# A decoder block's first stage in four groups of 256 tokens instead of two of 512, with plain fp32 projections

## The chip, the cores and the metric

The kernel runs on one core of one Trainium2 chip. The metric is device time in microseconds (us), the median of several timed runs. Beside them one execution was recorded by the hardware profiler; all rows below come from that one.

## What is computed

For 1024 tokens of 1024 features, in fp32 (the weights are drawn at random; shapes matter here, not values):

```
h    = modulate(rms_norm(x), shift1, scale1)      # shift, scale, gate: six rows made from c @ w_ada
q_g,k_g,v_g,a,r_g,q_s,k_s,v_s = split(h @ w_in)   # 1024 -> 2320 columns
o_gla = gated linear attention(q_g,k_g,v_g,a), normed, * silu(r_g)
o_swa = sliding-window attention(q_s,k_s,v_s), 8 heads, window 128, normed
x    = x + gate1 * (concat(o_gla,o_swa) @ w_out)
h2   = modulate(rms_norm(x), shift2, scale2)
for each of 8 heads of q = h2 @ w_q:               # 1024 -> 2048 columns
    16 best of 128 keys in each half, 16 best of their sums -> 16 experts e, gates g = softmax
a    = gelu(h2 . u_tab[e]);  out = sum_e g * a * v_tab[e]      # 128 experts of 16384 per token
x    = x + gate2 * out;  result = rms_norm(x) * final_g
```

## The kernel before

Tokens are held in 8 blocks of 128. The work has two stages.

**First stage** (`prelude(g)`, a generator with two `yield`s, so in three parts). It is run for two groups of 512 tokens (`GT`, `GB = 4` blocks). Part 1 normalises x, transposes it to `hT` and projects it. Part 2 is both attentions (`level`, `swa`), the v and r projections, the out-projection (`w_out`) and h2 with its transpose `h2T`. Part 3 multiplies by `w_q` and picks the 16 best experts of each head (`sel_head`, VectorE instructions L536 to L540, sums on GpSimd L552), then decodes them to expert numbers (`sel_decode4`).

Weights arrive in chunks of 256 columns, four tiles of 256 KB each (`load_chunk`). Two forms of product are in use. In group 0, and for `w_q` in both groups, the weights and `hT` are split into two fp32r parts (tile `whl`, made by ScalarE, VectorE and GpSimd at L165 and L166) and each product is three matmuls (`mm3`, L174 to L176). The other products of group 1 are one plain fp32 matmul on the tile as loaded (`wful`, L184 and L195). `proj_T` keeps the weights stationary and streams all tokens of the group (512 columns), `proj_tok` keeps 128 tokens stationary and streams 256 weight columns.

**Second stage** (the experts). Blocks 0 to 3 are *gathered*: for each of 128 slots, GpSimd gathers one row of `u` per token (512 KB, L631), VectorE takes the dot product with the token's row `h2s` (L632, tile `acts`); then one row of `v` per slot, which is either added up on VectorE (`gather_v`, L645 and L647) or contracted on TensorE (`gather_vt`, L699 and L674, tile `py`). The token rows come from DRAM: h2 is spilled to `h2d`, read back, transposed to `h2r`, and read from there. All gathered rows share the pool `gp` of seven 4 KB buffers. Blocks 4 to 7 are *dense*: all 16384 experts are computed for their 512 tokens in 128 tiles (`dense_u`: tiles `ur`, `uh`, matmuls `da`; `dense_w`, `dense_v`: tiles `wl`, `vl`, matmuls `dv` and `keep`) with a gate matrix that `build_gates` makes first (tile `st`, matmuls `gt`). 31 of the 128 `da` tiles are made ahead, some before and some during `build_gates`, and kept in DRAM (`gad`).

**What sets the order.** The program is written as one sequence: group 0; part 1 and 2 of group 1; u of block 0; v of block 0 with u of block 1; part 3 of group 1; `da` tiles; gates; v of 1 with u of 2; v of 2 with u of 3; v of 3; finish; dense loop. A scheduler then places the instructions of all engines by priority, so later work moves up beside earlier work; on each engine the order is fixed when the program is built.

Of the kernel before, what the change touches and what calls it, by code (L numbers as in the profile page):

```python
# [34 lines left out]
GBUF = 7  # L35
# [7 lines left out]
def hymba_peer_kernel(ctx, tc, x, c, w_adaT, b_adaT, g1T, g2T, w_in, w_alpha, b_alphaT,  # L43
# [56 lines left out]
    def row_of(dst, part):  # L100
        rep = wt("rep", [128, 8, 128], "e", 2)
# [12 lines left out]
    def late_consts():  # L114
# [8 lines left out]
        t = wt("lvlf", [128, NL, 128], "e", 2)  # L123
# [29 lines left out]
    def load_chunk(src, ci):  # L153
        res = []
        if busy[0] and src is not w_q:
            for kq in range(4):
                raw = wp.tile([128, 2, 256], F, name="wful", tag="whl", bufs=5)
                last_load[0] = SP.dma_start(raw, src[ci, kq // 2][:, kq % 2 * 2:kq % 2 * 2 + 2])
                res.append(raw)
            return res  # L160
        for kq in range(4):
            raw = wp.tile([128, 2, 256], F, name="wraw", tag="wraw", bufs=3)
            last_load[0] = SP.dma_start(raw, src[ci, kq // 2][:, kq % 2 * 2:kq % 2 * 2 + 2])
# [6 lines left out]
    busy = [False]  # L170
# [18 lines left out]
    def proj_tok(ch, hT, b, evac):
        p = pst("pK", "pj")  # L190
        for k in range(8):
            wk = ch[k // 2]
            ts = slice(b * 128, b * 128 + 128)
            if wk.dtype == F:
                PE.matmul(p[:, :256], lhsT=hT[:, k, ts], rhs=wk[:, k % 2], start=k == 0, stop=k == 7)  # L195
                continue
            mm3(p[:, :256], (hT[:, 0, k, ts], hT[:, 1, k, ts]), (wk[:, 0, k % 2], wk[:, 1, k % 2]), k == 0, k == 7)
        evac(p[:, :256])

    def transpose_split(blocks, hT, k, mul, add=None, spill=None, kind="ps", full=False):  # L200

        p = pst("tr", kind)
        for i, a in enumerate(blocks):
            PE.transpose(p[:, i * 128:(i + 1) * 128], a, ident)
        if full:
            if add is None:
                A.activation(hT[:, k], p, AF.Copy, scale=mul)
            else:
                A.activation(hT[:, k], p, AF.Identity, scale=mul, bias=add)
            return  # L210
        t = w2.tile([128, GT], F, name="trt", tag="w2")
# [624 lines left out]
    with ExitStack() as pre:  # L836
# [8 lines left out]
        for _ in prelude(0):  # L845
            pass
# [118 lines left out]
```

## Time and profile before

| | us |
|---|---|
| timed runs, median (lowest to highest of 3) | 2974.2 (2973.9 to 2984.5) |
| profiled execution, its own time | 2984.96 |
| span of its instructions | 2983.2 |
| TensorE (PE) busy / VectorE (DVE) busy | 2550.9 / 2342.1 |
| GpSimd (POOL) / ScalarE (ACT) busy | 1645.1 / 968.3 |
| granted TensorE clock, mean share | 0.917 |

Two kinds of view matter below. A table of stretches gives for each stretch of time the busy time of every engine: the stretch less PE's busy time is PE's idle time. A table of groups gives the price of one kind of instruction. The stretches were cut where the stages change: group 0's attention and out-projection end at about 335 us, its expert choice at 500; group 1's attention ends at about 860 and its choice at 1110; the gates are built from 1190 to 1494; the dense loop runs from 1560 to 2825.

### The profile page before, as it was taken

What the parts mean: (1) busy time and instruction counts of PE and PEld (TensorE: products, weight loads), DVE (VectorE), ACT (ScalarE), POOL (GpSimd) and SP (SyncE); (2) the same over time, 40 slices, a digit from 0 to 9 for tenths busy, and PEclk for the clock granted to TensorE, in tenths of its full rate; (3) what the DMA queues carried; (4) which work ended last, traced back from release to release, by engine and by line L of the source; (5) the groups of instructions that cost most, each with busy time, mean ns of one, the idle gap of its engine ahead of it and who ended that gap; (6) DMA issues with size and microseconds to landing.
All of it is one profiled execution on the core that took longest, in us unless ns stands there. A gap on an engine that the chain in (4) does not pass through costs nothing. (4 is left out here: it accounts for less than half of the span.)

```text
span 2983.2 us, 37273 instructions
## 1 busy us (share of the span) xinstructions
PE 2550.9 (86%) x12528; PEld 1960.1 (66%) x12528; DVE 2342.1 (79%) x5034; ACT 968.3 (32%) x1837; POOL 1645.1 (55%) x1551
## 2 busy tenths in 40 slices
PE   5799898898789873899769999999999999999800
PEld 4588775576566551688647777777888788877600
DVE  7754499899769999788846665666888888898987
ACT  4444533223132121577822222222222222222101
POOL 2321363678778888543244545454555555555675
PEclk9899999996889885999979999999999999999955
DMA  9502422689998787988798989998999999999897
GB/s 329 174 30 75 158 73 71 207 295 321 339 371 283 264 310 240 363 307 334 311 369 328 349 328 326 362 332 312 376 340 339 345 344 342 337 341 336 297 357 289
DMA packets 280657, 865.21 MB, mean 290 GB/s; under 512 B 28544, under 2 KB 69776, under 8 KB 278416
## 3 DMA queue, kind: packets, MB, share of 16 engines
q0 software_dynamic: 150192, 546.90, 50.6%
q1 hardware_dynamic: 122288, 271.10, 25.5%
q10 hardware_dynamic: 7984, 44.83, 3.8%
q8 instruction: 98, 1.61, 0.2%
q14 instruction: 95, 0.78, 0.1%
HBM read 806.36 MB, written 56.89 MB: 289 GB/s over the span
## 5 line engine op out<-in xcount | busy, mean ns | idle before, releaser
L631 POOL DMA_INDIRECT u<-in_peer_u_dram,exi x512 | 640.5, 1251 | 419.9 <-DVE acts L632 112.9
L632 DVE CUSTOM_DVE_ANT_0 u<-u,h2s 128x1024 f32<-128x1024 f32 x512 | 636.0, 1251 | 105.3 <-DMA u<-in_peer_u_dram,exi 64.7
L699 POOL DMA_INDIRECT v<-in_peer_v_dram,exs x256 | 300.7, 1175 | 278.0 <-DVE acts L632 137.2
L645 POOL DMA_INDIRECT v<-in_peer_v_dram,exi x256 | 332.0, 1297 | 219.8 <-DVE acts L632 124.1
L174 PE MATMUL da<-h2T,uh 128*128 128x512 f32 x1024 | 407.2, 398 | 6.3 <-ACT ga L781 6.0
L176 PE MATMUL da<-h2T,uh 128*128 128x512 f32 x1024 | 407.6, 398 | 4.6 <-DVE uh L775 4.4
L175 PE MATMUL da<-h2T,uh 128*128 128x512 f32 x1024 | 405.9, 396 | 0.0
L647 DVE SCALAR_TENSOR_TENSOR yacc<-v,gates,yacc 128x1024 f32<-128x1024 f32 x254 | 325.9, 1283 | 14.1 <-DMA v<-in_peer_v_dram,exi 10.8
L174 PE MATMUL dv<-vl,wl 128*128 128x512 f32 x640 | 251.4, 394 | 9.7 <-ACT vl L803 9.2
L176 PE MATMUL dv<-vl,wl 128*128 128x512 f32 x640 | 250.8, 392 | 0.0
L175 PE MATMUL dv<-vl,wl 128*128 128x512 f32 x640 | 249.6, 392 | 0.3 <-DVE vl L804 0.3
L822 DVE TENSOR_TENSOR acc<-dv,acc 128x512 f32<-128x512 f32 x155 | 105.1, 687 | 170.9 <-PE dv L176 153.3
L176 PEld LDWEIGHTS da<-h2T,uh 128*128 128x128 f32 x1024 | 194.4, 190 | 62.8 <-issue 12.6
L174 PEld LDWEIGHTS da<-h2T,uh 128*128 128x128 f32 x1024 | 194.7, 190 | 59.0 <-ACT ga L781 10.7
L175 PEld LDWEIGHTS da<-h2T,uh 128*128 128x128 f32 x1024 | 194.3, 190 | 51.4 <-issue 10.9
L674 PE MATMUL py<-v,wz 128*32 128x512 f32 x1024 | 152.0, 668 | 81.4 <-DMA v<-in_peer_v_dram,exs 81.3
L803 ACT ACTIVATE vl<-vr 128x1024 fp32r<-128x1024 f32 x128 | 132.8, 1051 | 251.9 <-PE dv L176 228.4
L774 ACT ACTIVATE uh<-ur 128x1024 fp32r<-128x1024 f32 x128 | 135.0, 1055 | 217.2 <-PE da L176 164.6
L781 ACT ACTIVATE ga<-da 128x512 f32<-128x512 f32 x128 | 76.0, 594 | 387.4 <-PE da L176 339.0
L166 POOL TENSOR_TENSOR whl<-wraw,whl 128x512 fp32r<-128x512 f32 x76 | 105.1, 1389 | 147.5 <-ACT whl L165 143.9
L775 DVE TENSOR_TENSOR uh<-ur,uh 128x1024 fp32r<-128x1024 f32 x128 | 162.1, 1267 | 26.9 <-ACT uh L774 22.8
L804 DVE TENSOR_TENSOR vl<-vr,vl 128x1024 fp32r<-128x1024 f32 x128 | 155.6, 1219 | 27.9 <-ACT vl L803 26.6
(278 smaller groups left out, 5435.9 us busy)
## 6 DMA issues: line engine op xcount, KB each, us to landing
ur<-in_peer_uT_dram SPq DMA_DIRECT2D x128, 512.0 KB
vr<-in_peer_v_dram SPq DMA_DIRECT2D x128, 512.0 KB
gd<-st ACTq DMA_DIRECT2D x16, 2048.0 KB
gl<-gd SPq DMA_DIRECT2D x32, 1024.0 KB
wada<-in_w_adaT_dram SPq DMA_DIRECT2D x48, 512.0 KB
wraw<-in_w_q_dram SPq DMA_DIRECT2D x64, 256.0 KB
wraw<-in_w_in_dram SPq DMA_DIRECT2D x40, 256.0 KB
wful<-in_w_in_dram SPq DMA_DIRECT2D x40, 256.0 KB
```

The costliest lines, as they stand in the source:

```text
L174: PE.matmul(p, lhsT=lh[0], rhs=rh[0], start=first, stop=False)
L175: PE.matmul(p, lhsT=lh[0], rhs=rh[1], start=False, stop=False)
L176: PE.matmul(p, lhsT=lh[1], rhs=rh[0], start=False, stop=last)
L631: GP.indirect_dma_start(out=u, out_offset=None, in_=peer_u, in_offset=bass.IndirectOffsetOnAxis(ap=exi[:, j:j + 1], axis=0))
L632: V.tensor_tensor_reduce(out=u, in0=u, in1=h2s, scale=1.0, scalar=0.0, op0=AL.mult, op1=AL.add, accum_out=a[:, j:j + 1])
L645: GP.indirect_dma_start(out=v, out_offset=None, in_=peer_v, in_offset=bass.IndirectOffsetOnAxis(ap=exi[:, j:j + 1], axis=0))
L647: V.scalar_tensor_tensor(out=y, in0=v, scalar=wg[:, j:j + 1], in1=y, op0=AL.mult, op1=AL.add)
L674: m = PE.matmul(py[q:q + 32, :], lhsT=wz[:, j, i % 8 * 32:i % 8 * 32 + 32], rhs=vs[j][:, hf * 512:hf * 512 + 512], start=i == 0, stop=i == 31)
L699: gi = GP.indirect_dma_start(out=v, out_offset=None, in_=peer_v, in_offset=bass.IndirectOffsetOnAxis(ap=exs[:, t:t + 1], axis=0))
L774: A.activation(hl[:, 0], u, AF.Copy)
L775: V.tensor_tensor(hl[:, 1], u, hl[:, 0], AL.subtract)
L804: V.tensor_tensor(vl[:, 1], v, vl[:, 0], AL.subtract)
```

## The change

Groups are now of 256 tokens (`GB = 2`), so the first stage runs four times (p0 to p3), each with all weights loaded again. All its products are plain fp32: `load_chunk` keeps the loaded tile (six buffers), the split and its three-matmul form remain only in the dense stage. The gathered blocks are 0, 1 (from p0) and 6, 7 (from p3), the dense ones 2 to 5 (p1 and p2), whose split `h2D` is written as soon as h2 is there. The token rows of gathered blocks stay in SBUF (`h2rows`, two buffers); `h2d` and `h2r` are gone. `gp` has six buffers. The order is a list: `PLAN` (p is the next part of a group, d decodes, u gathers u, w is `gather_vt`, a6 six `da` tiles), and after the gates `POST` (x is `gather_v`). `finish` is as before, for blocks 0, 1, 6, 7.

```diff
-GT = 512
-GB = GT // 128
-NG = S // GT
-
-D0 = 4
+
+GB = 2
+GT = GB * 128
+
+D0 = 2
 ND = 4
...
-GBUF = 7
+GBUF = 6
...
     def load_chunk(src, ci):
...
         for kq in range(4):
-            raw = wp.tile([128, 2, 256], F, name="wraw", tag="wraw", bufs=3)
-            last_load[0] = SP.dma_start(raw, src[ci, kq // 2][:, kq % 2 * 2:kq % 2 * 2 + 2])
-            hl = wp.tile([128, 2, 2, 256], R, name="whl", tag="whl", bufs=5)
-            A.activation(hl[:, 0], raw, AF.Copy)
-            (GP if kq % 2 or (not busy[0] and src is w_q) else V).tensor_tensor(hl[:, 1], raw, hl[:, 0], AL.subtract)
-            res.append(hl)
+            w = wp.tile([128, 2, 256], F, name="wful", tag="w", bufs=6)
+            last_load[0] = SP.dma_start(w, src[ci, kq // 2][:, kq % 2 * 2:kq % 2 * 2 + 2])
+            res.append(w)
...
     def proj_T(ch, hT, mt, evac):
-        p = pst("pT", "pj")
+        p = pst("pT", "pj")[:, :GT]
         for k in range(8):
...
-            mm3(p, (wk[:, 0, k % 2, cs], wk[:, 1, k % 2, cs]), (hT[:, 0, k], hT[:, 1, k]), k == 0, k == 7)
+            PE.matmul(p, lhsT=ch[k // 2][:, k % 2, mt * 128:mt * 128 + 128], rhs=hT[:, k], start=k == 0, stop=k == 7)
...
-        for blk in range(D0):
-            h2 = gp.tile([128, 8, 128], F, name="h2l", tag="g")
-            SP.dma_start(h2, h2d[:, :, blk * 128:blk * 128 + 128].rearrange("k p t -> p k t"))
-            h2s = gp.tile([128, D], F, name="h2t", tag="g")
+    def token_rows(h2T, g):
+
+        for b in range(GB):
+            h2s = h2rows[g * GB + b] = sm.tile([128, D], F, name="h2s", tag="h2s", bufs=2)
...
+    PLAN = "p0 p0 p0 p1 d0 p1 u0 w0 p1 p2 d1 p2 u1 p2 p3 d2 p3 p3 d3 a6".split()
+    POST = "w1 u6 x6+u7 x7".split()
...
-    run(gather_vt(1, sels[1]), gather_u(2, sels[2]))
-    run(gather_v(2, sels[2]), gather_u(3, sels[3]))
-    run(gather_v(3, sels[3]))
-    for b in range(D0):
+    for op in POST:
+        run(*(GATHER[o[0]](int(o[1:]), sels[int(o[1:])]) for o in op.split("+")))
+    for b in GATHERED:
         finish(None, b, GP)
```

Two places show what the scheduler made of it. The first is GpSimd where the gathers of u begin. In the rows before, `cand` is part of the expert choice, `oh` of the decoding, `e` of an attention level, `h2s` the load of the token rows.

```order
91 L552 TENSOR_TENSOR cand<-tv 128x16 x50
92 L576 TENSOR_TENSOR oh<-oh,dif 128x1024
...
96 L627 DMA h2s<-h2r 128x1024
97 L576 TENSOR_TENSOR oh<-oh,idf 128x1024
98 L576 TENSOR_TENSOR oh<-oh,dif 128x1024 x2
99 L576 TENSOR_TENSOR oh<-oh,idf 128x1024
100 L322 TENSOR_TENSOR e<-bcum 128x8x64
101 L322 TENSOR_TENSOR e<-bcum 128x16x32
102 L325 TENSOR_TENSOR e<-e,kg 128x8x64
103 L325 TENSOR_TENSOR e<-e,kg 128x16x32
104 L631 DMA u<-in_peer_u_dram,exi 128x1024 x9
```

The same place now:

```order
38 L532 TENSOR_TENSOR cand<-tv 128x16 x28
39 L556 TENSOR_TENSOR oh<-oh,dif 128x1024
40 L556 TENSOR_TENSOR oh<-oh,idf 128x1024
41 L298 TENSOR_TENSOR e<-bcum 128x4x64
42 L298 TENSOR_TENSOR e<-bcum 128x8x32
43 L556 TENSOR_TENSOR oh<-oh,dif 128x1024
44 L556 TENSOR_TENSOR oh<-oh,idf 128x1024
45 L607 DMA u<-in_peer_u_dram,exi 128x1024 x4
46 L301 TENSOR_TENSOR e<-e,kg 128x4x64
47 L607 DMA u<-in_peer_u_dram,exi 128x1024 x2
```

Before, 160 `cand` rows (the choice for 512 tokens) stand ahead of the first gather; now 80 do (256 tokens), and the gathers begin in the second group's attention as they did before, only that this group comes earlier.

The second place is VectorE at the end of the program, where `yacc` adds one gathered row of v, `acc` belongs to the dense loop and `ga`, `wl`, `vl` prepare its last tiles. Before:

```order
3613 L804 TENSOR_TENSOR vl<-vr,vl 128x1024
3614 L647 SCALAR_TENSOR_TENSOR yacc<-v,gates,yacc 128x1024
3615 L822 TENSOR_TENSOR acc<-dv,acc 128x512 x2
3616 L647 SCALAR_TENSOR_TENSOR yacc<-v,gates,yacc 128x1024 x3
3617 L822 TENSOR_TENSOR acc<-dv,acc 128x512
...
3621 L822 TENSOR_TENSOR acc<-dv,acc 128x512
3622 L647 SCALAR_TENSOR_TENSOR yacc<-v,gates,yacc 128x1024 x80
3623 L725 TENSOR_TENSOR yl<-yl,rows 128x1024
```

and now:

```order
3591 L772 TENSOR_TENSOR ga<-gl,ga 128x512
3592 L623 SCALAR_TENSOR_TENSOR yacc<-v,gates,yacc 128x1024
3593 L775 TENSOR_TENSOR wl<-ga,wl 128x512
3594 L623 SCALAR_TENSOR_TENSOR yacc<-v,gates,yacc 128x1024 x4
3595 L798 TENSOR_TENSOR acc<-dv,acc 128x512 x2
3596 L623 SCALAR_TENSOR_TENSOR yacc<-v,gates,yacc 128x1024 x4
3597 L798 TENSOR_TENSOR acc<-dv,acc 128x512
3598 L623 SCALAR_TENSOR_TENSOR yacc<-v,gates,yacc 128x1024 x2
3599 L798 TENSOR_TENSOR acc<-dv,acc 128x512
3600 L701 TENSOR_TENSOR yl<-yl,rows 128x1024
3601 L623 SCALAR_TENSOR_TENSOR yacc<-v,gates,yacc 128x1024
3602 L798 TENSOR_TENSOR acc<-dv,acc 128x512
```

Eighty gathered rows stood behind the last instruction of the dense loop; now twelve stand behind the last `ga`, among the loop's last additions.

## Rows read from the trace of the kernel before

**Rows 1.** The page: busy time; DMA share in 40 slices; bytes moved.

```profile
PE 2550.9 (86%) x12528; PEld 1960.1 (66%) x12528; DVE 2342.1 (79%) x5034; ACT 968.3 (32%) x1837; POOL 1645.1 (55%) x1551
DMA  9502422689998787988798989998999999999897
DMA packets 280657, 865.21 MB, mean 290 GB/s; under 512 B 28544, under 2 KB 69776, under 8 KB 278416
```

**Rows 2.** Stretches: start:end, length, busy time (instructions) by engine, clock, DMA.

```profile
core 0: us, PE busy (x) PEld busy (x) DVE busy (x) ACT busy (x) POOL busy (x), PEclk, DMA share, GB/s
0.00:45.00 45.00, 15.24 (x59) 12.07 (x60) 32.59 (x50) 23.67 (x36) 18.04 (x17) 1.00 0.83 303
45.00:335.00 290.00, 257.28 (x1711) 221.19 (x1710) 164.52 (x362) 129.60 (x306) 75.79 (x57) 0.92 0.39 133
335.00:500.00 165.00, 149.38 (x681) 118.94 (x682) 144.34 (x801) 64.40 (x121) 86.29 (x194) 0.93 0.25 82
500.00:566.00 66.00, 57.20 (x153) 25.97 (x151) 58.38 (x126) 20.02 (x32) 34.90 (x23) 0.95 0.42 135
566.00:860.00 294.00, 251.82 (x1237) 194.70 (x1237) 239.57 (x516) 77.43 (x217) 221.81 (x178) 0.83 0.90 321
860.00:1110.00 250.00, 219.30 (x1042) 152.21 (x1042) 231.34 (x902) 73.78 (x129) 210.30 (x278) 0.92 0.85 297
1110.00:1190.00 80.00, 29.71 (x122) 11.52 (x123) 73.78 (x174) 8.86 (x30) 66.53 (x56) 0.53 0.72 241
1190.00:1494.00 304.00, 276.54 (x1734) 221.80 (x1732) 248.83 (x679) 211.75 (x490) 117.81 (x99) 0.97 0.87 330
1494.00:1560.00 66.00, 38.28 (x167) 24.85 (x166) 32.20 (x48) 13.86 (x20) 31.80 (x27) 0.74 0.97 373
1560.00:2825.00 1265.00, 1256.13 (x5637) 976.84 (x5635) 983.64 (x1266) 335.88 (x444) 676.46 (x528) 1.00 0.92 337
2825.00:2983.00 158.00, 0.00 (x0) 0.00 (x0) 132.92 (x115) 9.06 (x16) 105.38 (x98) 0.50 0.88 322
```

**Rows 3.** Order of time on DVE: start, length, instruction; the last gathered rows.

```profile
2937.75 2.61 DVE L647 SCALAR_TENSOR_TENSOR yacc<-v,gates,yacc 128x1024 f32<-128x1024 f32 x2 [0.21 <-DMA v<-in_peer_v_dram,exi]
```

**Rows 4.** One stretch, instructions with tile whl alone: PE, PEld, DVE, ACT, POOL.

```profile
0.00:1560.00 1560.00, 378.85 (x1848) 296.44 (x1848) 33.94 (x44) 74.03 (x120) 105.08 (x76) 0.89 0.69 248
```

**Rows 5.** The same stretch, tile wful alone: PE, PEld.

```profile
0.00:1560.00 1560.00, 213.90 (x720) 138.75 (x720) 0.89 0.69 248
```

**Rows 6.** Groups: names, shapes, count | busy us, mean ns | idle before, releaser.

```profile
L195 PE MATMUL pK<-wful,hT 128*128 128x256 f32 x320 | 85.0, 412 | 1.3 <-DVE pa L265 1.3
L184 PE MATMUL pT<-hT,wful 128*128 128x512 f32 x144 | 65.6, 607 | 8.8 <-ACT qs L304 7.3 <-ACT kg L278 1.5
L195 PE MATMUL pK<-wful,cT 128*128 128x256 f32 x256 | 63.3, 401 | 8.2 <-DVE y L492 6.4 <-DMA wful<-in_w_out_dram 1.6 <-issue 0.2
L525 PE MATMUL sk<-kk,qT 128*128 128x128 f32 x256 | 42.5, 290 | 12.3 <-ACT s L527 9.9 <-ACT qT L521 2.3
L674 PE MATMUL py<-v,wz 128*32 128x512 f32 x1024 | 152.0, 668 | 81.4 <-DMA v<-in_peer_v_dram,exs 81.3
L774 ACT ACTIVATE uh<-ur 128x1024 fp32r<-128x1024 f32 x128 | 135.0, 1055 | 217.2 <-PE da L176 164.6 <-DMA ur<-in_peer_uT_dram 37.4 <-DVE acc L822 14.3
L775 DVE TENSOR_TENSOR uh<-ur,uh 128x1024 fp32r<-128x1024 f32 x128 | 162.1, 1267 | 26.9 <-ACT uh L774 22.8 <-ACT whl L165 2.9 <-issue 1.0
```

**Rows 7.** Order of time on PE: a run of 256-column fp32 matmuls.

```profile
776.91 1.89 PE L195 MATMUL pK<-wful,cT 128*128 128x256 f32 x8
```

**Rows 8.** A stretch of split 256-column matmuls, tile whl alone.

```profile
280.00:325.00 45.00, 42.66 (x363) 41.56 (x362) 4.28 (x5) 7.21 (x12) 9.84 (x7) 1.00 0.40 136
```

**Rows 9.** The choice of group 1, instructions with tile u alone: DVE, POOL.

```profile
860.00:1110.00 250.00, 69.90 (x53) 60.61 (x52) 0.92 0.85 297
```

**Rows 10.** DMA issues: a weight tile's size.

```profile
wful<-in_w_out_dram SPq DMA_DIRECT2D x16, 256.0 KB
```

More of the change, by code (lines that the diff above doesn't have):

```diff
@@ L22 @@
 NB = S // 128
-GT = 512
-GB = GT // 128
-NG = S // GT
-D0 = 4
+GB = 2
+GT = GB * 128
+D0 = 2
 ND = 4
 DT = ND * 128
+GATHERED = [b for b in range(NB) if not D0 <= b < D0 + ND]
 NGA = NB - ND
@@ L187, in proj_T @@
         evac(p)
     def proj_tok(ch, hT, b, evac):
-        p = pst("pK", "pj")
+        p = pst("pK", "pj")[:, :256]
         for k in range(8):
[L192 to L197, printed above, removed]
@@ L198, in proj_tok, with transpose_to @@
-        evac(p[:, :256])
-    def transpose_split(blocks, hT, k, mul, add=None, spill=None, kind="ps", full=False):
-        p = pst("tr", kind)
+            PE.matmul(p, lhsT=hT[:, k, b * 128:b * 128 + 128], rhs=ch[k // 2][:, k % 2], start=k == 0, stop=k == 7)
+        evac(p)
+    def transpose_to(blocks, hT, k, mul, add=None, split=None, kind="ps"):
+        p = pst("tr", kind)[:, :GT]
         for i, a in enumerate(blocks):
             PE.transpose(p[:, i * 128:(i + 1) * 128], a, ident)
[L205 to L211, printed above, removed]
@@ L212, in transpose_split @@
         if add is None:
-            A.activation(t, p, AF.Copy, scale=mul)
+            A.activation(hT[:, k], p, AF.Copy, scale=mul)
         else:
-            A.activation(t, p, AF.Identity, scale=mul, bias=add)
-        A.activation(hT[:, 0, k], t, AF.Copy)
-        V.tensor_tensor(hT[:, 1, k], t, hT[:, 0, k], AL.subtract)
-        if spill is not None:
-            SP.dma_start(spill, t)
+            A.activation(hT[:, k], p, AF.Identity, scale=mul, bias=add)
+        if split is not None:
+            A.activation(split[:, 0, k], hT[:, k], AF.Copy)
+            V.tensor_tensor(split[:, 1, k], hT[:, k], split[:, 0, k], AL.subtract)
@@ L248, in prelude @@
                     mod_in(k)
-                transpose_split([xn[b][:, k * 128:(k + 1) * 128] for b in range(GB)], hT, k, A1[:, k:k + 1], modT[:, k:k + 1], kind="lv", full=g > 0)
+                transpose_to([xn[b][:, k * 128:(k + 1) * 128] for b in range(GB)], hT, k, A1[:, k:k + 1], modT[:, k:k + 1], kind="lv")
         qg = wt("qg", [128, 2, GT])
@@ L500, in prelude @@
             A.activation(ys[b], ys[b], AF.Copy, scale=rsqrt_of(ss, D, "n2"))
-        h2T = hx.tile([128, 2, 8, GT], R, name="h2T", tag="hT")
+        h2T = Parts([wt("h2T", [128, 2, GT], tag, n) for tag, n in (("ST0", 1), ("ST1", 1), ("e", 2), ("e", 2))])
+        dense = D0 <= g * GB < D0 + ND
+        split = h2D[:, :, :, (g * GB - D0) * 128:(g * GB - D0) * 128 + GT] if dense else None
         for k in range(8):
-            transpose_split([ys[b][:, k * 128:(k + 1) * 128] for b in range(GB)], h2T, k, A2[:, k:k + 1], modT[:, 24 + k:25 + k], None if g else h2d[k])
+            transpose_to([ys[b][:, k * 128:(k + 1) * 128] for b in range(GB)], h2T, k, A2[:, k:k + 1], modT[:, 24 + k:25 + k], split)
+        if not dense:
+            token_rows(h2T, g)
         if g == 0:
-            t = wt("g2row", tag="e", bufs=2)
+            t = wt("g2row", tag="oh", bufs=2)
             row_of(t, 5)
@@ L532, in prelude @@
         res[g] = sels
-        h2Ts[g] = h2T
     def top16(s, v, i, n):
@@ L886, in hymba_peer_kernel @@
         build_gates(lists)
-        lq.close()
-        for i in tiles[N1:]:
+        for i in tiles:
             ahead(i)
+    dq.close()
+    lq.close()
+    du = ctx.enter_context(tc.tile_pool(name="du", bufs=2, side="right", reuse_waits="tile"))
     dv = ctx.enter_context(tc.tile_pool(name="dv", bufs=1, reuse_waits="tile"))
```

175 lines of the change are left out of this document (80 added, 95 removed).

## The prediction

> **What bounds the kernel now.** I read the page's totals first, then the stretches, then the prices of single instructions. TensorE is the busiest engine with 2550.9 us, VectorE follows with 2342.1, and the DMA engines are seven to nine tenths busy from the ninth of 40 slices on, after an early hole [rows 1]. No engine is full over the whole span, so the stretches decide [rows 2]. In the dense loop (1560 to 2825) PE is idle for 9 us of 1265: there PE sets the pace. Behind it lie 158 us without one matmul. Gathered rows are still being added there; the last two end at 2940.4 [rows 3], and some 43 us of finishing follow. Ahead of the loop PE is idle for 265 us, spread over all stages. So the profiled time, 2985.0, is PE's work (2551), plus its idle time before its last matmul (9 + 265 = 274), plus the tail (158), plus 2 around the span. I predict each of these. The profiled execution is 10.7 us above the median of the timed runs, 2974.2; I sum on the former and subtract 10.7.
>
> **PE's work.** In the built programs `da`, `dv`, `keep`, `gt`, `py`, transposes and attention matmuls are the same in number (3072, 1920, 1152, 512, 512 for the first five); only the projections change. Removed: 378.9 us of split matmuls [rows 4] and 213.9 us of plain ones [rows 5], 593 together. Added: 1376 plain fp32 matmuls of 256 columns. Their prices: 85.0 us for 160 of them with `hT` gives 0.531 each, 63.3 for 128 with `cT` 0.495 (each leaves two records, so x320 is 160) [rows 6]. 320 with `hT` make 170 us and 256 with `cT` 127. The other 800 are `proj_T` at 256 columns, which no row shows. Half of its 512-column price (65.6 / 72 = 0.911) is 0.456, the lower end; 0.531 is the upper end, since the columns are the same. I take 0.495, the row between: 396 us (365 to 425). Sum 693 (662 to 722), so PE's work grows by **100 us** (69 to 129).
>
> A clean run of four such matmuls takes 1.89 us, 0.47 each [rows 7]; a split one of 256 columns takes 42.66 / 363 = 0.118 per matmul, 0.353 for three [rows 8]. The Trainium skill, FP8 and Floating Point Precision, TensorE Precision Notes, says that true fp32 goes through the array in four passes; four times 0.118 is 0.47, so the trace agrees, and the rule speaks against this change. By the rule alone the 1376 would take 647 us and the work would grow by 54 instead of 100. I keep the rows, which hold the gaps of a real stage.
>
> **The tail.** VectorE's order now leaves 12 gathered additions behind the last `ga`, among the loop's last `acc`, where 80 stood behind the last `acc`. Then the same finishing follows as before, 43 us, of which the loop's last additions hide nothing. I take 45 for 158: **-113 us**. Bounds: 30, if dense finishing overlaps the gathered one, and 120, if some 50 gathers are late at (2940.4 - 2825) / 80 = 1.45 us each.
>
> **PE's idle time, stage by stage** [rows 2]. In us, before and then after:
> Start (0 to 45): 30, then 30; the same 16 tiles of `w_ada` must land.
> Group 0 (45 to 335): 33, then 17, as it is half the attention.
> Its expert choice (335 to 500): 16, then 8.
> Projections of the next group (500 to 566): 9, then 9.
> Attention beside gathers (566 to 860): 42; then the same density of gathers, for 512 tokens in p1 and p3 (72 and 81 of u in VectorE's order), 45, and p2, which has none of u, as group 0, 17: 62.
> Choice of group 1 beside gathers (860 to 1110): 31. This is now the dearest point. A choice for 512 tokens keeps VectorE busy for 144.3 us of 165 (335 to 500), so 72 for 256. One u costs it 69.90 / 53 = 1.32 us [rows 9]. The order puts 56 of u between the last out-projection and the last choice of p1, and 47 in p3: 146 and 134 us on VectorE. PE has 128 matmuls at 0.495, 32 scores at 42.5 / 128 = 0.33 [rows 6] and some transposes, 78 us. It waits for VectorE through the five buffers of the scores (tile `s`), so it can be five of the 16 score blocks ahead, 45 and 42 us; in these it makes the next projections, or `da` tiles, which stand next in its queue. Idle then 23 and 14; without any lead 68 and 56. p2 has only w0 beside it (PE 108, VectorE 72): 8. I take 57 (45 to 132).
> Decoding (1110 to 1190): 50, then 0. The lists of the dense blocks now come with d1 and d2, hidden by the attention of p2 and p3; d3 is hidden by six `da` tiles. Without that cover it is 25 for two blocks.
> Gates (1190 to 1494): 27, then 30. The 81 us for which PE waits on gathered v [rows 6] fall mostly here and in the row before last; w1 now runs alone and GpSimd is not held by u, so I take half of them, 14 of 27, away. The six `da` tiles have one buffer each, so the split of the next tile is not hidden behind the last: 6 times 1.06 + 1.27 us [rows 6] and a little, 16.
> Change of pools (1494 to 1560): 28, then 28. Dense loop: 9, then 9.
> The sums are 275 and 250: **-25 us** (-37 to +75).
>
> **Edits that I cost at nothing.** The splits (74 us ACT, 105 POOL, 34 DVE [rows 4]) go, on engines with room beside PE. 176 more weight tiles of 256 KB [rows 10] are 46 MB; at 337 GB/s 137 us of DMA, hidden in p0 and p1, where the DMA engines are 0.25 to 0.42 busy [rows 2]. The first gather comes at about 45 + 145 + 83 (start, half of two stretches) + 25 (a quarter of the fp32 growth) + 30 for decoding = 330 us. Without that cover: of 865 MB [rows 1] + 46 - 8 for the spill that is gone, about 850 come after it (48 tiles of `w_ada` and p0's weights lie ahead); at 337 GB/s they end at 2850, some 90 us before the forecast's end. Six instead of seven row buffers: GpSimd's 528 instructions in the loop, nearly all gathers, are one per 2.4 us, so six buffers leave 14 us for each row; nothing, or up to 20.
>
> **Sum.** 2985.0 + 100 - 113 - 25 = 2947, less 10.7: **2936 us**. Its own range, 2890 to 2985, holds the prices' bounds and the ordinary scatter of the idle terms.
>
> **The rivals.**
> *Starved in the choice* (slower). PE has no lead in p1 and p3, because the next instructions in its queue wait for VectorE too, and stands there for 68 + 56 + 8 = 132 instead of 57. With d3 uncovered (+25) and 0.531 for the 800 (+29) the time is 2936 + 75 + 25 + 29 = 3065; without the last two 3011. It is slower from about 2936 + 38, so once these stages leave PE idle for over 95 us. For it: in 1110 to 1190 PE was idle 50 of 80 us behind VectorE. Against it: in 860 to 1110, with 53 of u beside the choice [rows 9], PE was 88% busy [rows 2].
> *The gaps close* (faster). Waits for gathered v and decoding made 131 of the 274; if both go wholly and p1 to p3 run as tightly as group 0, idle falls to 180: 2866. For it: w0 and w1 run alone. Against it: the same u stand beside half as many columns per stage.
> *Late rows.* The dense loop ends but gathers don't: 50 left cost 75 us more than my tail, 3011. For it: VectorE's order has 500 rows in the loop, and the DMA share there was 0.92. Against it: the old loop carried 528 instructions of GpSimd with PE at 99% [rows 2].
>
> **How the numbers follow.** Forecast 0.52, starved 0.20, gaps close 0.16, late rows 0.12. A measurement can't tell less than 0.5%, 15 us, from no change. Of the forecast's 0.52 some 0.36 lie below 2959, 0.13 within 15 us of 2974, 0.03 above; so faster 0.36 + 0.16 + a little of the others' low ends, 0.54; same 0.16; slower 0.30. The range reaches into the rivals: 2862 to 3035.
>
> **What would show it.** PE busy at about 2650 and `wful` at about 693 us; the first u near 330 us; no stretch like 1110 to 1190; PE's last matmul within 50 us of the end; idle in the choices of p1 and p3 of 40 us. I am wrong if PE's work grows by over 130, if these choices leave PE idle for over 95 us, or if rows are still gathered well after the last matmul.

## The result, and the profile after

The changed kernel took 2937.35 us (median of 4 runs, 2932.59 to 2944.7), the kernel before 2974.82 in the same session: a ratio of 0.987, with an interval of 0.984 to 0.990. Forecast were 2936 us. The profiled execution took 2935.2 us with a span of 2933.4. It splits into TensorE's work 2618.0, its idle time before the last matmul 270.7, the tail 44.7 and 2 around the span. Before, these were 2551, 274, 158 and 2.

The page's totals of the kernel after, to be held against [rows 1]:

```profile
PE 2618.0 (89%) x12704; PEld 2061.1 (70%) x12704; DVE 2270.2 (77%) x5027; ACT 942.6 (32%) x1844; POOL 1567.0 (53%) x1499
...
DMA  9533689979987999778898989999999999999986
```

TensorE has 67 us more work, VectorE 72 less, and the early hole in the DMA row is shorter. The stretches of the same kernel, with the columns of [rows 2]: the start; then, for each of the four groups in turn, the stretch up to the end of its out-projection and the stretch of its choice (eight rows); gates; change of pools; dense loop; tail.

```profile
0.00:45.00 45.00, 17.57 (x50) 12.08 (x51) 26.80 (x47) 18.15 (x29) 14.31 (x13) 0.92 0.93 331
45.00:197.00 152.00, 139.19 (x721) 113.62 (x720) 83.23 (x201) 47.64 (x131) 15.87 (x19) 0.96 0.57 204
197.00:284.00 87.00, 77.19 (x403) 67.73 (x403) 52.52 (x290) 28.61 (x64) 22.59 (x62) 0.94 0.41 135
284.00:470.00 186.00, 157.79 (x747) 126.10 (x745) 155.25 (x427) 48.44 (x130) 119.80 (x118) 0.86 0.78 270
470.00:570.00 100.00, 73.75 (x357) 62.83 (x358) 88.27 (x348) 30.65 (x71) 69.42 (x92) 0.86 0.96 347
570.00:792.00 222.00, 191.39 (x1085) 126.17 (x1083) 122.79 (x380) 57.01 (x157) 147.20 (x162) 0.94 0.87 308
792.00:904.00 112.00, 101.12 (x541) 66.38 (x538) 68.89 (x374) 30.71 (x68) 68.27 (x120) 0.93 0.84 304
904.00:1084.00 180.00, 157.13 (x777) 125.47 (x776) 156.49 (x358) 49.75 (x136) 138.19 (x112) 0.88 0.87 306
1084.00:1193.00 109.00, 78.72 (x376) 66.76 (x376) 92.22 (x353) 22.18 (x52) 74.20 (x99) 0.86 0.90 322
1193.00:1627.00 434.00, 380.63 (x2257) 275.24 (x2257) 287.32 (x843) 243.60 (x537) 188.39 (x186) 0.94 0.83 304
1627.00:1670.00 43.00, 24.30 (x75) 18.08 (x76) 21.97 (x33) 8.18 (x12) 15.55 (x13) 0.70 1.01 392
1670.00:2889.00 1219.00, 1219.00 (x5327) 1000.61 (x5325) 1081.60 (x1347) 348.54 (x448) 675.10 (x487) 1.00 0.93 336
2889.00:2934.00 45.00, 0.24 (x2) 0.00 (x0) 32.82 (x36) 9.19 (x16) 18.15 (x18) 0.53 0.59 208
```

The first column less the second is TensorE's idle time of a stretch. The loop begins 110 us later than before (1670 for 1560), takes 46 less, and only 45 us follow it for 158. (Before, 59.7 us of `py` matmuls stood in the loop; now none do.) The choices of groups 1 and 3 (470 and 1084) leave TensorE idle for 26.3 and 30.3 us. Where in them, the order of time on TensorE tells, group 1 first (start, length, instruction, idle time before it and what ended it):

```profile
488.54 0.90 PE L188 MATMUL tr<-ident,y 128*128 128x128 f32 x3 [18.85 <-ACT y L477]
...
1104.24 0.90 PE L188 MATMUL tr<-ident,y 128*128 128x128 f32 x3 [20.72 <-ACT y L477]
```

Two waits make 39.6 of the 56.6 us. They stand before the choice begins: the out-projection is done and the normalised rows `y` are not there. What is late is seen on VectorE, and on SyncE's queue, both between 461 and 482:

```profile
469.38 0.43 DVE L470 TENSOR_TENSOR y<-y,xr 128x256 f32<-128x256 f32 x1 [2.17 <-DMA xr<-in_x_dram]
...
471.54 0.47 DVE L470 TENSOR_TENSOR y<-y,xr 128x256 f32<-128x256 f32 x1
...
476.51 0.08 DVE L608 DVE_READ_ACCUMULATOR2_ANT acts<- 128x1 f32 x1
481.23 0.43 DVE L470 TENSOR_TENSOR y<-y,xr 128x256 f32<-128x256 f32 x1 [4.64 <-DMA xr<-in_x_dram]
```

```profile
461.87 6.20 SPq L153 DMA_DIRECT2D wful<-in_w_q_dram  x4
469.84 0.33 SPq L468 DMA_DIRECT2D xr<-in_x_dram  x1
470.22 0.42 SPq L153 DMA_DIRECT2D wful<-in_w_q_dram  x1
472.04 0.33 SPq L468 DMA_DIRECT2D xr<-in_x_dram  x1
```

VectorE adds the slice `xr` of the residual at 481.23, after waiting for it. `xr` has two buffers, and the two last slices were asked for at 469.84 and 472.04, just when the additions of the two slices before them were done (469.81 and 472.01). Five weight tiles of 256 KB for the next projections had been asked for ahead of the first, a sixth ahead of the second. The first slice was used 11.4 us after it was asked for, the second landed after 12.3. The DMA engines are 96% busy in the stretch from 470 to 570. From the addition to the scaled `y` another 7 us pass.

The projections after, by shape (to [rows 4 to 6]; their sum over the first 1700 us is 681.4):

```profile
L175 PE MATMUL pT<-h2T,wful 128*128 128x256 f32 x1024 | 249.7, 391 | 0.1
...
L181 PE MATMUL pK<-wful,hT 128*128 128x256 f32 x640 | 164.7, 406 | 2.8 <-ACT hT L192 2.8
...
L175 PE MATMUL pT<-hT,wful 128*128 128x256 f32 x576 | 142.5, 405 | 16.5 <-ACT kg L254 7.8 <-ACT qs L280 4.1 <-DMA wful<-in_w_in_dram 2.7
...
L181 PE MATMUL pK<-wful,cT 128*128 128x256 f32 x512 | 124.6, 397 | 7.9 <-DVE y L469 6.7 <-DMA wful<-in_w_out_dram 1.0
```

Halved counts give 0.488 us (249.7 / 512), 0.515, 0.495 and 0.487 for one matmul; the forecast had 0.495 for the `pT`, 0.531 and 0.495 for the `pK`.

### The profile page after: what moved, and what is told of

It is laid out like the page before. It is cut to its first block, busy times and chain, and to the rows that moved or that the text cites. A ratio compares the mean times of both kernels' runs of the same rounds, so it can differ in the third digit from the quotient of the medians.

```text
span 2933.4 us, 37844 instructions
## 1 busy us (share of the span) xinstructions
PE 2618.0 (89%) x12704; PEld 2061.1 (70%) x12704; DVE 2270.2 (77%) x5027; ACT 942.6 (32%) x1844; POOL 1567.0 (53%) x1499
## 4 chain that ended last, share of the span: by engine, by line
PE 67%; DVE 15%; DMA 8%; issue 4%; POOL 3%; ACT 2%; SPq 0%; POOLq 0%; ACTq 0%; DVEq 0%
PE da L162 8%; PE da L160 8%; PE da L161 8%; PE dv L160 5%; PE dv L161 5%; PE dv L162 5%; PE pK L181 5%; PE pT L175 4%; DVE u L608 4%; PE gt L738 3%; PE py L650 3%; PE keep L160 3%; PE keep L161 3%; PE keep L162 3%; DMA v<-in_peer_v_dram,exs 2%
## 5 line engine op out<-in xcount | busy, mean ns | idle before, releaser
L607 POOL DMA_INDIRECT u<-in_peer_u_dram,exi x512 | 652.4, 1274 | 453.9 <-DVE acts L608 316.1
L621 POOL DMA_INDIRECT v<-in_peer_v_dram,exi x256 | 366.5, 1432 | 288.4 <-DVE yacc L623 233.9
L162 PE MATMUL da<-h2D,uh 128*128 128x512 f32 x1024 | 410.7, 401 | 28.1 <-DVE uh L751 28.1
L160 PE MATMUL da<-h2D,uh 128*128 128x512 f32 x1024 | 412.0, 402 | 9.8 <-ACT uh L750 9.8
L675 POOL DMA_INDIRECT v<-in_peer_v_dram,exs x256 | 261.5, 1022 | 295.7 <-PE py L650 236.2
L161 PE MATMUL da<-h2D,uh 128*128 128x512 f32 x1024 | 410.3, 401 | 0.0
L162 PEld LDWEIGHTS da<-h2D,uh 128*128 128x128 f32 x1024 | 196.8, 192 | 79.1 <-DVE uh L751 32.6
L175 PE MATMUL pT<-h2T,wful 128*128 128x256 f32 x1024 | 249.7, 391 | 0.1
L160 PEld LDWEIGHTS da<-h2D,uh 128*128 128x128 f32 x1024 | 197.1, 192 | 61.0 <-ACT uh L750 13.8
L161 PEld LDWEIGHTS da<-h2D,uh 128*128 128x128 f32 x1024 | 196.9, 192 | 48.4 <-issue 6.7
L175 PEld LDWEIGHTS pT<-h2T,wful 128*128 128x128 f32 x1024 | 192.8, 197 | 30.3 <-issue 7.5
L774 ACT ACTIVATE wl<-ga 128x512 fp32r<-128x512 f32 x128 | 80.0, 626 | 336.1 <-PE dv L162 249.0
L650 PE MATMUL py<-v,wz 128*32 128x512 f32 x1024 | 141.8, 624 | 29.6 <-DMA v<-in_peer_v_dram,exs 29.6
L738 PEld LDWEIGHTS gt<-o,o 128*128 128x128 f32 x1024 | 132.4, 198 | 50.1 <-issue 16.3
L181 PE MATMUL pK<-wful,hT 128*128 128x256 f32 x640 | 164.7, 406 | 2.8 <-ACT hT L192 2.8
## 6 DMA issues: line engine op xcount, KB each, us to landing
gd<-st ACTq DMA_DIRECT2D x16, 2048.0 KB, 15.5
```

The costliest lines, as they stand in the source:

```text
L160: PE.matmul(p, lhsT=lh[0], rhs=rh[0], start=first, stop=False)
L161: PE.matmul(p, lhsT=lh[0], rhs=rh[1], start=False, stop=False)
L162: PE.matmul(p, lhsT=lh[1], rhs=rh[0], start=False, stop=last)
L175: PE.matmul(p, lhsT=ch[k // 2][:, k % 2, mt * 128:mt * 128 + 128], rhs=hT[:, k], start=k == 0, stop=k == 7)
L181: PE.matmul(p, lhsT=hT[:, k, b * 128:b * 128 + 128], rhs=ch[k // 2][:, k % 2], start=k == 0, stop=k == 7)
L607: GP.indirect_dma_start(out=u, out_offset=None, in_=peer_u, in_offset=bass.IndirectOffsetOnAxis(ap=exi[:, j:j + 1], axis=0))
```

## The experiments

All times are medians. "The changed kernel" is 2937.35 us; the kernel before took 2974.82 to 2983.6 beside these runs, and each ratio is to it as run beside them. TensorE's idle time is that before its last matmul, and the tail what follows; both, and TensorE's work, are of the run's profiled execution. The kernel before took about 2975 us beside `xr4`, `xract`, `a0`, `gbuf5` and the changed kernel itself, and 2981 to 2984 beside the others, so a difference between runs of the two sets is sure to some 10 us only; the ratios show it without this shift.

**Four buffers for the slices** (`xr4`):

```diff
-                xt = wt("xr", [128, 256], "xr", 2)
+                xt = wt("xr", [128, 256], "xr", 4)
-        ex = w2.tile([128, 128], F, name="ex", tag="ex", bufs=2)
+        ex = w2.tile([128, 128], F, name="ex", tag="ex", bufs=1)
```

> The changed kernel with four buffers instead of two for the residual slices `xr` (the space comes from one buffer of the small list `ex`). Theory 1 (late slices): the 18.9 and 20.7 us for which TensorE stands before the transposes of `y` at the end of groups 1 and 3 come from slices that are asked for behind five weight tiles; with four buffers they are asked for two steps earlier, the two gaps fall to about 4 us each and TensorE's idle time from 271 to about 240. VectorE's order has 6 gathered additions behind the last `acc` where the changed kernel has none, so the tail grows from 44 to about 54: some 2915 in all. Theory 2 (VectorE): the gaps stay, since dots of `u` stand ahead of the norm in VectorE's order; idle above 260, time 2930 to 2940. Theory 3 (rows set the end): idle falls by 30 and the tail grows by as much, because the loop starts earlier with more rows left; 2930 to 2940 with another split.

Measured: 2920.1 us (0.982, 0.979 to 0.985), 17 less than the changed kernel. VectorE no longer waits for `xr` at all, but the gaps ahead of `tr` fell only to 14.2 and 10.7: another wait stood behind the first. The order of time on TensorE, and on ScalarE:

```profile
482.69 0.90 PE L188 MATMUL tr<-ident,y 128*128 128x128 f32 x3 [14.18 <-ACT y L477]
```

```profile
481.49 1.15 ACT L477 ACTIVATE y<-y,n2r 128x1024 f32<-128x1024 f32 x1 [10.43 <-DMA x1d<-y]
```

ScalarE scales `y` in place and must wait until its store to `x1d` has read it; that store was issued at 469 behind six weight tiles. Idle time fell by 7 (forecast 31), the tail grew by 11 (forecast 10). The choices of groups 1 and 3 had 24 us less idle time, but nearly as much came back at the six early `da` tiles, which waited longer for VectorE's halves:

```profile
1164.61 0.80 PE L162 MATMUL da<-h2D,uh 128*128 128x512 f32 x1 [12.32 <-DVE uh L751]
...
1203.69 0.79 PE L162 MATMUL da<-h2D,uh 128*128 128x512 f32 x1 [29.13 <-DVE uh L751]
```

What made the run faster is TensorE's work, 2596.5 for 2618.0, which no theory had; the last section says where such differences come from. So theory 1 holds for the wait for `xr` and for the tail, not for the gaps, the idle time and the source of the gain.

**The slices on another queue** (`xract`):

```diff
-                with tc.issue_after(last_load[0].ins):
-                    SP.dma_start(xt, x[...])
+                    A.dma_start(xt, x[...])
```

> The changed kernel with `xr` loaded by ScalarE's queue instead of SyncE's, two buffers as before. If standing in SyncE's queue behind the weight tiles makes the slices late, the two gaps before the transposes of `y` fall from 18.9 and 20.7 to under 10 each and the time by 15 to 25, to about 2915. If the full DMA engines (share 0.96 to 0.97 there) or the two buffers make them late, the gaps stay within 5 us and the time within 8 of 2937.

Measured: 2950.0 us (0.991, 0.988 to 0.994), 13 more than the changed kernel and outside the forecast of either case; the gaps were 18.7 and 16.6, as the second case has them. The slices of group 1 were again asked for only when the additions two steps before were done (472.27 and 473.80, after 471.85 and 473.66), so the two buffers and not the queue set when they are asked for. What they then waited for the run doesn't separate: VectorE's recorded waits for `xr` fell from 15.2 us to 0.3, but its order had more dots of `u`, waiting for rows themselves, ahead of the addition, which came at 481.09 for 481.23. The Trainium skill, DMA: Bandwidth & Descriptors, Issuing engines are not separate DMA queues, says that transfers of all issuing engines run interleaved on the same 16 DMA engines; the nearly unchanged gaps are in keeping with it and don't show it.

**No early `da` tiles** (`a0`):

```diff
-    PLAN = "... p3 p3 d3 a6".split()
+    PLAN = "... p3 p3 d3".split()
```

> The changed kernel without the six `da` tiles that are made while d3 is decoded; all 31 are made in the stage of the gates. The prediction had these tiles hide 25 us of decoding and cost 16 by themselves. By it TensorE's idle time between the last scores and the first `gt` is about 25 to 35 (26 now), and the time 5 to 15 us above 2937. Rival: TensorE waits there for VectorE's halves of the tiles and not for the decoding, so that without them the stretch is shorter by the tiles' work and the whole kernel is 5 to 20 us faster.

Measured: 2936.2 us (0.987, 0.983 to 0.991): no difference, which neither side had forecast. TensorE's idle time is 22 more, the tail 12 less, its work 10 less. Between the last scores and the first `gt` it is idle for 63 us (forecast 25 to 35), 36 of them in one wait and 26 in waits of `py` for gathered v. None is for decoding:

```profile
1205.54 0.47 PE L641 MATMUL wp<-ident,gates 128*128 128x128 f32 x1 [36.01 <-DVE gates L612]
```

This transpose is the first instruction of w1 and waits for the last of the 128 dots of u1, of which 13 were left behind the last scores. So the prediction's sentence that the tiles hide decoding named the wrong wait; they hide the end of u1.

**Five row buffers** (`gbuf5`): `GBUF = 6` becomes 5.

> The changed kernel with five row buffers instead of six. VectorE's order then has 25 gathered additions behind the last `acc` and 36 behind the last `ga`, where the changed kernel has none and 12. Theory 1 (buffers set the pace of the rows, and rows left set the tail): the tail grows by 25 x 1.45 = 36 us, to about 80, and the time to about 2970; then six for seven was no free edit either. Theory 2 (a buffer less costs nothing, as the prediction had it for six): time within 10 of 2937.

Measured: 3021.4 us (1.015, 1.011 to 1.020), 84 more than the changed kernel and more than either theory had. The tail grew by 48 to 93, idle time by 30. The first multiplication of u1's gates came at 1277.6 for 1209.6, the last `py` at 1697.6 for 1573.3. So rows are late ahead of the loop, too, not only behind it.

**Six row buffers in the kernel before** (`b6`): `GBUF = 7` becomes 6 there.

> The kernel before with six row buffers instead of seven, nothing else: one part of the change alone. VectorE's order leaves 97 gathered additions behind the last `acc` instead of 80. Theory 1 (a buffer costs through the rows left): 17 x 1.45 = 25 us more of tail and a little more of idle time, 2995 to 3015. Theory 2 (the prediction: nothing, or up to 20): 2970 to 2990. Theory 3 (as dear as from six to five in the changed kernel): 3055.

Measured: 3001.0 us, 1.0056 of the kernel before beside it (1.0040 to 1.0073), some 17 us. Tail 190 for 158, idle 274 as before. Theory 1 in sign and place; of the "nothing, or up to 20" of the prediction, the upper end.

**Seven row buffers** (`a0_gbuf7`): `a0` with `GBUF = 7`, and one buffer for `acts` to make room.

> The kernel of the run without the six early `da` tiles (2936 us; that frees the space), with seven row buffers instead of six. Theory 1 (each buffer less slows the gathered rows, 84 us from six to five): the way from six to seven gives some of it back. VectorE's order has 206 dots of `u` in the loop for 226 and no addition behind the last `ga` for 5; the waits of `py` for gathered rows shrink, idle time falls by 10 to 25, the tail by no more than 5: 2910 to 2925. Theory 2 (the prediction: the step between six and seven costs nothing): 2928 to 2945. Theory 3 (the step is worth as much as that from five to six): below 2880.

Measured: 2932.8 us (0.983, 0.982 to 0.985), in the range of theory 2; by the ratios it is 11 us below `a0`, between the two ranges, so the time decides little. The tail went from 32 to 18, and idle time from 293 to 279, the latter as theory 1 has it, but TensorE's work, of the same instructions, rose from 2608 to 2633, at a mean granted clock of 0.934 for 0.939. u1 ended at 1158.8, ahead of the last scores. These came later, at 1243 for 1170, since the order has more beside them. The stretch up to group 3's out-projection, in `a0`, then here:

```profile
899.00:1067.00 168.00, 152.48 (x796) 119.86 (x794) 145.28 (x345) 49.38 (x138) 124.61 (x108) 0.94 0.90 319
```

```profile
898.00:1130.00 232.00, 176.35 (x759) 141.90 (x757) 208.47 (x527) 50.10 (x135) 178.96 (x162) 0.77 0.87 305
```

VectorE has 108 dots of `u` in it for 68, and TensorE is idle for 56 us for 16. The rows came earlier and cost there what they gave behind.

**Projections twice** (`qtwice`):

```diff
-        for k in range(8):
+        for k in list(range(8)) * n:   # n = 2 for w_q of groups 1 and 3
             PE.matmul(p, lhsT=..., rhs=hT[:, k], start=k == 0, stop=k == 7)
```

> The changed kernel with every `w_q` projection of groups 1 and 3 computed twice into the same bank (the first result is thrown away): 256 more plain fp32 matmuls in just the two choices that the rival has starved by VectorE, 256 x 249.7 / 512 = 125 us of TensorE's work. Theory 1 (TensorE sets the pace of these choices; its idle time there is the wait for the slices ahead of them): nothing takes the work up but some rows gathered in the meantime, the tail can fall from 44 to about 32, so 3040 to 3060. Theory 2 (rival: VectorE sets the pace of the choices): half of it or more hides, 2990 or less.

Measured: 3052.5 us (1.023, 1.021 to 1.025), 115 more for an estimate of 125 (107 by the ratios). TensorE's work rose by 140 (109 of it in the projections), idle time by 6, and the tail fell from 45 to 17. The page's totals of it:

```profile
PE 2758.4 (90%) x13216; PEld 2175.3 (71%) x13216; DVE 2262.1 (74%) x5027; ACT 940.9 (31%) x1845; POOL 1522.5 (50%) x1499
```

TensorE takes nearly all of the added work on the path: theory 1. VectorE did not starve the choices that have gathers beside them.

**w1 and u6 in turn** (`pair`):

```diff
-    POST = "w1 u6 x6+u7 x7".split()
+    POST = "w1+u6 x6+u7 x7".split()
```

> The changed kernel with the rows of w1 taken in turn with those of u6, as the kernel before paired its blocks, instead of w1 ahead of them. TensorE's order then has 140 of the 512 matmuls with gathered v behind the loop's first (none in the changed kernel, 236 before), VectorE's 12 gathered additions behind the last `acc` and 24 behind the last `ga` (0 and 12; 80 and 96 before). Rows left at the start of the loop: 199 + 256 + 70 = 525 for 487 (625 before). Theory 1 (the rows left at the loop's start set the tail): tail 44 + 12 x 1.45 = 61, time 2950 to 2960. Theory 2 (the earlier first gather made the tail short, and the pairing does not matter): tail 44, time within 8 of 2937.

Measured: 2955.6 us (0.992, 0.989 to 0.994; its profiled execution, 2971, is at the upper end of its runs, with 20 us more of TensorE's work). Tail 62 for the forecast 61, with the first gather where it was: the rows left for the loop set the tail. Over all runs it goes with the number of gathered additions that VectorE's order has behind its last `acc`: none, 17 to 45 us, and the shorter the earlier the last of them ends (1.8 us behind the last matmul in the changed kernel, 87 ahead of it in `qtwice`); 6 (`xr4`), 56; 12, 62; 25 (`gbuf5`), 93; 80 (before), 158; 97 (`b6`), 190.

**The two waits for stores and slices taken away** (`a0_xr4_yn`): `a0` with four buffers for `xr`, and

```diff
-            A.activation(ys[b], ys[b], AF.Copy, scale=...)
+            yn = wt(f"yn{b}")
+            A.activation(yn, ys[b], AF.Copy, scale=...)
+            ys[b] = yn
```

> The kernel without the six early `da` tiles (2936 us), with four buffers for `xr` and the normalised rows written to tiles of their own, so that ScalarE's scaling (L477) no longer waits for the store of `y` to `x1d`. In the run with four buffers alone the gaps ahead of the transposes of `y` were still 14.2 and 10.7 us, and there ScalarE waited for that store. Theory 1 (slices, then the store, each behind weight tiles): both gaps fall to 4 or less, TensorE's idle time from 293 to about 260, some of it gone to the tail (4 additions behind the last `ga`, as many as without): 2900 to 2915. Theory 2 (VectorE's dots hold the norm up): the gaps stay above 9 and the time at 2915 to 2930.

Measured: 2957.1 us (0.991, 0.988 to 0.993), 21 more than `a0`, or 11 by the ratios, whose intervals overlap: neither theory. The gaps ahead of `tr` are down to 7.4 and 8.0 (forecast 4 or less), yet idle time is 301 for 293, and TensorE's work 2623 for 2608.

**The same with seven row buffers** (`best`):

> The same with seven row buffers, which alone moved the time by nothing but took the tail to 18 us. Theory 1 (the two edits add up: idle from the gaps, tail from the buffers): 2885 to 2905. Theory 2 (the rows taken earlier stand beside TensorE's work ahead of the loop and cost there what they give at the end, as with seven buffers alone): as the run with six buffers, within 8 of it.

Measured: 2874.9 us (0.965, 0.963 to 0.968), 82 less for one buffer, where the same step without the two edits had been worth 3 (11 by the ratios). Neither theory had it. Of the difference between the two profiled executions, 36 us are TensorE's work, 35 its idle time and 13 the tail. TensorE's order of time in `a0_xr4_yn`, then in `best`, shows 20 of the idle time:

```profile
1161.57 1.22 PE L508 MATMUL sk<-kk,qT 128*128 128x128 f32 x4 [3.81 <-ACT s L510]
1235.86 0.47 PE L643 MATMUL wp<-ident,gates 128*128 128x128 f32 x1 [73.07 <-DVE gates L614]
```

```profile
1132.45 1.23 PE L508 MATMUL sk<-kk,qT 128*128 128x128 f32 x4 [4.32 <-ACT s L510]
1186.40 0.47 PE L643 MATMUL wp<-ident,gates 128*128 128x128 f32 x1 [52.72 <-DVE gates L614]
```

With six buffers u1 ends at 1235.5; TensorE, faster by the edits, comes to w1 at 1163 and stands for 73 us. With seven u1 ends at 1186.1. Two chains meet at w1, TensorE's stages and the gathered rows. In `a0_gbuf7` TensorE was the later, in `a0_xr4_yn` the rows. How long TensorE stands there goes with the dots of u1 that are left behind the last scores: none in `a0_gbuf7`, 13 in `a0` (36.0 us), 24 in `best` (52.7) and 31 in `a0_xr4_yn` (73.1). That both edits are needed to move the meeting is an argument from these orders: each program's order was made anew, and `best` has 66 dots in the stretch up to group 3's out-projection where `a0_gbuf7` has 108. `best` ends with idle 266, tail 20, and work 2587 at a mean granted clock of 0.948. Why u1 ended 33 us later in `a0_xr4_yn` than in `a0` (1202.6) stays open.

**Split projections in groups 1 and 2** (`split12`): `a0` with one buffer less for `ex`, and

```diff
+            hl = wp.tile([128, 2, 2, 256], R, name="whl", tag="whl", bufs=4)
+            A.activation(hl[:, 0], raw, AF.Copy)
+            (GP if kq % 2 else V).tensor_tensor(hl[:, 1], raw, hl[:, 0], AL.subtract)
...
+            mm3(p, (ch[k // 2][:, 0, ...], ch[k // 2][:, 1, ...]), (h3[:, 0, k], h3[:, 1, k]), k == 0, k == 7)
```

> The kernel without the six early `da` tiles (2936 us; the space is used), with the `w_q` projections of groups 1 and 2 as three matmuls of split halves in place of one plain fp32 matmul: 256 of the 1376. ScalarE, VectorE and GpSimd split 64 weight tiles for it; the activations are at hand split. Theory 1 (plain fp32 costs TensorE time on the path): 256 x (0.488 - 0.353) = 35 us less work, hidden splits, 2895 to 2912. Theory 2 (the splits stand in the way of rows and choice, which is what plain fp32 bought): TensorE's work falls by 25 to 40 but idle time or tail take most of it back, 2925 to 2945. Theory 3 (slower): above 2945.

Measured: 2951.2 us (0.990, 0.988 to 0.993), 15 more than `a0`, or 10 by the ratios, whose intervals overlap. TensorE's work fell by 22, its idle time rose by 22 (17 of it waits of matmuls for VectorE's halves, 8 for GpSimd's), the tail by 9. The split matmuls alone, over 0 to 1700 (PE, PEld, DVE, ACT, POOL):

```profile
0.00:1700.00 1700.00, 113.55 (x768) 100.68 (x768) 32.93 (x32) 39.71 (x64) 41.26 (x32) 0.91 0.81 289
```

Three split matmuls take 113.55 / 256 = 0.444 us here, not the 0.353 of the clean stretch [rows 8], for 0.477 of one plain fp32 matmul in the same kernel (122.2 / 256). By these figures plain fp32 costs TensorE 7% more, and spares ScalarE, VectorE and GpSimd 114 us of splitting for these 256. Theory 2 in its mechanism; the time is in theory 3's range, but that the split form is slower is not clear of the noise.

**The early tiles put back into the fastest** (`best2`): `best` with `a6` in PLAN, `ur` from the row buffers (`gp.tile(..., tag="g")`) and the halves in the tile of `yn`.

> The fastest kernel so far (2874.9 us: seven row buffers, four buffers for `xr`, normalised rows in tiles of their own, no early `da` tiles) with the six early `da` tiles of the changed kernel put back; their input takes a row buffer and their split halves the tile of the normalised rows. In that kernel TensorE stands for 52.7 us after the last scores, until d3 is decoded and the pools change. Theory 1 (the six tiles, 33 us of TensorE's work, fill this as they do in the changed kernel, where 26 us of idle time are left in the stretch): idle time falls by 20 to 30, VectorE's order has 7 additions behind the last `ga` for none, tail up by 5: 2850 to 2862. Theory 2 (VectorE, busy with dots of `u`, makes the halves of the tiles late, as in the run with four buffers for `xr`, where TensorE waited 12.3 and 29.1 us for them): 2868 to 2882.

Measured: 2896.0 us (0.972, 0.968 to 0.977), 21 slower than `best`, of which the tail is 14 and idle time 5: neither theory. The tiles did not fill the wait: the first stood 43.2 us for ScalarE's half of an input that SyncE could ask for only at 1172.9, as its row buffer came free that late (the last is read from the edit, not from a row). TensorE:

```profile
1178.77 0.79 PE L160 MATMUL da<-h2D,uh 128*128 128x512 f32 x1 [43.24 <-ACT uh L753]
```

The fastest version is `best`, 2874.9 us.

## Why the prediction was right, step by step

The time was right within 2 us, but not all of its terms were: work and idle time missed by 33 and 22 us with opposite signs, and the correction at the end by another 13. What was right is the mechanism of the largest term, the tail, and the sign of the work; that the sum came out this close is luck.

**TensorE's work**: forecast +100 (69 to 129), measured +67. Its projections were +89 (592.8 to 681.4), inside the bounds, and the middle row was the right one for `pT`. The rest of the miss is an assumption never stated: that all else keeps its time. The other instructions, nearly the same in number, took 21.5 less. `py` fell from 152.0 [rows 6] to 141.8, since only 11 us of it ran at the lower clock for 35 before; the attention's groups fell by some 15 together, and `da` rose by 12. Where the rest lies was not followed. On the whole the clock did little here: TensorE was busy at the lower level for 206 us before and 200 after. The mean granted clock of the span rose from 0.917 to 0.941 mainly because the tail, at 0.50 without a matmul [rows 2], is shorter.

**The tail**: forecast -113 to 45, measured 44.7. The step was read from VectorE's order, and `pair`, `gbuf5` and `b6` show that this count is what sets it. The reading of the finishing held, too: the last gathered row ends with the loop, and 42.4 us follow it, for 43 forecast.

```profile
2889.75 1.28 DVE L623 SCALAR_TENSOR_TENSOR yacc<-v,gates,yacc 128x1024 f32<-128x1024 f32 x1
```

What makes the count smaller is seen in the traces: behind the loop's start stand 231 dots, 256 additions and none of w1's 128 rows, where before there were 245, 256 and 118 rows. `pair`, which leaves 70 of w1's rows to the loop, gives back 17 of the 113 us. That the rest comes from the earlier first gather was not tested alone.

**TensorE's idle time**: forecast -25, measured -3. Stage by stage, forecast and measured: start 30, 27; group 0 with its choice 25, 23; out-projections of groups 1 to 3 with the stretch ahead 71, 82; their choices 57, 67; gates 30, 53; pools 28, 19; loop 9, 0. The choices came within 10 us for the wrong reason. The five score buffers were said to leave 23 and 14 us in p1 and p3 behind VectorE's dots. In fact 39.6 stood ahead of the choices, where the normalised rows were late, and only 17 were the rest. These 39.6 begin with `xr`, a transfer that no row of before showed as late (1.2 us of waiting in all); with its wait gone (`xr4`) 24.8 were left, in which ScalarE waited 10.4 and 6.9 for the store of `y`. In the gates' stretch the prediction left 13 us of the old waits; measured were 16 of `py` for gathered v and 14 of `gt` for its inputs, and the halves of the `da` tiles cost 24 for 16.

The prediction also misread the rows of before: of the 50 us between 1110 and 1190 that it gave to decoding, 26.8 are `py` waiting for gathered v, and only 28.5 of the 81 us of such waits lie in the choice and the gates, where it had most of them. So the 131 us of its rival *the gaps close* hold some 27 us twice.

**Six row buffers**: "nothing, or up to 20" was near its upper end in the kernel before (17), and misleading as a rule: the next buffer cost 84, and one more in place brought 3 or 82, by what else the order held. The reckoning by 14 us for each row looked at the loop alone.

**The other edits at nothing**: the first gather came at 326 (forecast 330); the doubled weights cost no stretch of their own, though their tiles fill the DMA engines when `xr` is asked for. **The correction** by -10.7 from the profiled execution to the median did not hold for the new kernel, whose profile lies 2 below its median; that error of 13 offset the 12 that the sum of terms had too much.

**The rivals**: starved in the choice fell with `qtwice` and with 67 us of idle time in the choices of p1 to p3 where 95 were needed. The gaps did not close: waits for gathered v fell (`py`: 81 to 30 us), but new ones came. Late rows did not occur with six buffers, and are what happens with five.

## What to carry to other kernels

Where one engine sets the pace and a second chain (here gathered rows) must meet it, look for the places where they meet, and ask for each which comes later: here edits to one of them brought nothing or little, and two together far more than their sum, though the engines' orders changed with them. Small loads ahead of a normalisation need buffers enough to be asked for early (here four for two took VectorE's wait away), and what overwrites in place a tile that a store still reads waits for the store (10.4 us here), a wait that showed only when the one ahead of it was gone. The number of late instructions in an engine's order told the tail better than any rate did.

## What the runs showed of the hardware

Plain fp32 matmuls of 256 columns took 0.477 to 0.515 us in stages, and three split ones 0.444 (`split12`): far nearer than clean stretches suggest (0.47 and 0.353). Part of that is the clock: of the 113.6 us of split matmuls 15.5 ran at the lower level, of the 122.2 of plain ones 4.8. The Trainium skill, FP8 and Floating Point Precision, TensorE Precision Notes, gives true fp32 four passes, by which three split matmuls, of one pass each as the clean stretch has them, would take three quarters; the stage had 0.93.

After a wait TensorE ran at the lower of its two levels, 1.2 for 2.4 GHz, for a while. In the kernel after, an 11.2 us wait in the six tiles is followed by `da` matmuls of one a 0.43 us at a granted clock of 0.50 (1207 to 1212), and then of one a 0.23 us at 1.00 (from 1213):

```profile
1206.75 0.80 PE L162 MATMUL da<-h2D,uh 128*128 128x512 f32 x1 [11.21 <-DVE uh L751]
1207.34 0.63 PE L160 MATMUL da<-h2D,uh 128*128 128x512 f32 x1
1207.77 0.63 PE L161 MATMUL da<-h2D,uh 128*128 128x512 f32 x1
...
1212.36 0.39 PE L160 MATMUL da<-h2D,uh 128*128 128x512 f32 x1
```

TensorE's work differed by 50 us between kernels with the same instructions, 2587 (`best`) to 2638 (`pair`), and the mean granted clock with it, 0.948 to 0.932. The clock records of the traces let one add up how long TensorE was busy at the lower level: 151 us in `best`, 240 in `pair`. A `da` matmul takes about twice as long there, so half of that time, 75 and 120 us, is lost, and the difference of 45 is most of the 50. In all ten kernels with the instructions of the kernel after, the work less that half is 2511 to 2527 us. So the time at the lower clock accounts for nearly all of the difference in work, for that of `xr4` (154 us for 200) and of `best` against `a0_xr4_yn` (151 for 219) among them. That waits bring it down is seen in rows like those above; how much each wait costs beyond its length was not tested by itself.
